# A streaming encoder on one core: own buffers for the `up` copies, constants loaded in the mixers, and corrected durations in the order planner

## The chip, the cores and the metric

The kernel runs on one core of one Trainium2 chip. The metric is the device time of one execution in microseconds, lower is better. Three runs of the kernel before gave 2532.02, 2538.91 and 2546.72 us; the median, 2538.91, is the time before.

## What is computed

A two-layer encoder works on 576 token columns at once (512 of a prompt, 64 of a sample), all in 32-bit floats. Each layer has a gated feed-forward network (FFN), a token mixer and a second FFN, each with a modulated norm ahead of it and a gated residual behind it. In short:

```
for l in range(2):
    mod = (silu(c) @ ada_w[l] + ada_b[l])      # shift, scale, gate for 3 sub-layers
    x = x + 0.5 * gate * swiglu(norm(x), ff_w_in[l, 0], ff_w_out[l, 0])
    x = x + gate * mixer(norm(x))              # l = 0: gated delta rule + short conv
                                               # l = 1: stick-breaking attention
    x = x + 0.5 * gate * swiglu(norm(x), ff_w_in[l, 1], ff_w_out[l, 1])
y = rmsnorm(x)
swiglu(h) = (silu(h @ w_gate) * (h @ w_up)) @ w_out     # width 2816
```

The states and caches of both groups are outputs too.

## The kernel before

**Layout.** Activations are transposed: 128 features on the partitions, 576 token columns, in two halves of 288. A 32-bit product is made of three matmuls on split operands: the high part `wh` and the low part `wl` of a weight block, the high part `XH` and the low part `XL` of the activations (`wh XH + wh XL + wl XH`). In the FFN's second product the activations are `HH` and `HL`. One matmul has 128 x 128 weights and 288 columns. Weights come as `stage` tiles over the sync queue; ScalarE copies the high part, VectorE, GpSimd or an accumulating DMA makes the low part.

**Stages.** FFN 0, mixer 0 (four pairs of delta-rule heads, a chain of small matmuls per pair), FFN 1, FFN 2, mixer 1 (eight pairs of attention heads, nine query blocks each), FFN 3. In each FFN the 22 input steps come in three chunks of 8, 8 and 6, and after each chunk 8 output products, with a residual addition (`x<-d,mod,x`) on VectorE.

**Two kinds of input step.** A *whole step* (`dense`) makes gate and up of 128 hidden features with 2 x 8 blocks x 2 halves x 3 = 96 matmuls. A *step of seven* (`dense7`) makes the same with a scheme of seven block products, 7 x 4 x 3 = 84 matmuls, in the order P1, P2, P6, P5, P7, P3, P4; it needs sums of weight blocks (`ss`, VectorE) and sums of activations (`TH`, `TL`, made once per FFN by `t_task`). P1, P6, P7 and P4 accumulate on one PSUM bank with copies (`sg`, `up`) taken in between; P5 and P3 accumulate on another, and the copy of P5 is taken between them. `PLAIN` says how many steps of each FFN, from the first on, are whole.

**The buffers around the change.** In a step of seven, `evac7` copies P5 into the first half of an `hm` tile and P7 into the only `up` tile; `hm` has one buffer, and holds the product of gate and up of the step before until `HH` (ScalarE) and `HL` (VectorE) are made from it, which `late` puts into the next step, behind P6 and P5.

**Modulation.** The 2 x 72 columns of `mod` are products of a broadcast vector `cb` with rows of `ada_w`, on VectorE: a tile (`ada_tile`) is one 512 KB load `aw` over the sync queue into one of two buffers and two products `jk<-aw,cb` of 128 x 1024, one per group. `ada_task` gives out a tile every so many planned ns (6200 in FFN 0, 9500 in FFN 1 and 2) and not before the planned VectorE is nearly through.

**What sets the order.** The program is written out in the order in which a planner meets it. `Model` keeps a planned clock for each engine; `Eng.cost` gives each instruction a duration from its size. `Sched` holds tasks (the chains of the mixers, the norms, `t_task`, `ada_task`); after every third dense matmul `tick` runs the tasks whose time the planned TensorE clock has reached. A task gives back the planned time at which its data is ready. So the durations in `Eng.cost` decide behind how many dense matmuls each small step of a chain is placed, and where the modulation tiles stand on VectorE; each engine then runs its list strictly in that order. `S.until` and `S.finish` move the planned clock forward where the dense work needs a task's result.

All instructions are issued by one helper, line 191 of the profile, so groups are told apart by the tile names: `d` and `a` are PSUM tiles, `cm` holds the identity and the masks, `raw`, `kq`, `nat`, `uu`, `ot` belong to the delta chain, `qbH`, `kH`, `sg`, `cp`, `wt`, `vtk` to attention.

## Time and profile before

| | |
|---|---|
| median of three runs | 2538.91 us |
| the profiled execution, by its own time | 2543.82 us |
| its span in the profile | 2542.1 us |
| TensorE busy | 2377.7 us (94%) |
| VectorE busy | 1789.1 us (70%) |
| ScalarE busy | 1092.6 us (43%) |
| GpSimd busy | 340.5 us (13%) |
| mean granted clock of TensorE | 0.959 |

The profiled execution ran 4.9 us longer than the median of the runs. A busy share is the time between start and end of an engine's instructions; matmuls overlap, so a dense matmul shows about 300 ns although the next one starts much sooner. A wait of one engine costs time only where that engine sets the end; TensorE, in a list of its own, does so nearly everywhere. The granted clock has two levels, 1.0 (2.4 GHz) and 0.5 (1.2 GHz); a value between is a mean over a stretch.

### The profile page before, as it was taken

How to read it: one execution, taken by the hardware profiler on the slowest of the kernel's cores; microseconds unless marked ns; L12 is line 12 of the kernel's file. 1: busy time of each engine (PE TensorE's matmuls, PEld its weight loads, DVE VectorE, ACT ScalarE, POOL GpSimd, SP SyncE). 2: the span in 40 equal slices, each digit the busy share in tenths (PEclk: the TensorE clock that was granted, in tenths of full speed). 3: DMA queues.
4: the chain of work that ended last, by engine and by line, in shares of the span. 5: the costliest groups of instructions: out<-in, count | busy, mean ns of one | idle time of the engine just before them, and what ended most of it. 6: DMA issues, size and time to landing. Idle time of an engine off the chain costs nothing. (4 is left out here: it accounts for less than half of the span.)

```text
span 2542.1 us, 45405 instructions
## 1 busy us (share of the span) xinstructions
PE 2377.7 (94%) x18352; PEld 2287.6 (90%) x18352; DVE 1789.1 (70%) x3463; ACT 1092.6 (43%) x1990; POOL 340.5 (13%) x468
## 2 busy tenths in 40 slices
PE   6989899999888999999999999999988889999998
PEld 5989899998788999999999999999977879999998
DVE  7688978587686578686867756565576777848474
ACT  4434525453222255362544445354554445425252
POOL 4100000342122230000021000013000004000001
PEclk8989999998788999999999999999999989999999
DMA  6656655232123165464636544343544314423222
GB/s 237 191 163 175 191 178 150 88 109 57 45 58 104 44 164 158 145 188 150 174 107 174 150 113 136 100 117 109 159 127 128 105 63 137 127 83 100 92 88 75
DMA packets 107350, 321.55 MB, mean 126 GB/s; under 512 B 26066, under 2 KB 28370, under 8 KB 106884
## 3 DMA queue, kind: packets, MB, share of 16 engines
q1 hardware_dynamic: 95044, 273.02, 32.4%
q0 software_dynamic: 12096, 45.62, 9.7%
q8 instruction: 145, 2.38, 0.4%
q14 instruction: 65, 0.53, 0.1%
HBM read 261.47 MB, written 11.51 MB: 107 GB/s over the span
## 5 line engine op out<-in xcount | busy, mean ns | idle before, releaser
L191 PE MATMUL d<-XH,wh 128*128 128x288 f32 x2280 | 707.8, 310 | 53.5 <-ACT hm L191 36.5
L191 PE MATMUL d<-XL,wh 128*128 128x288 f32 x2280 | 690.9, 303 | 14.5 <-POOL XL L191 11.1
L191 PE MATMUL d<-XH,wl 128*128 128x288 f32 x2280 | 689.3, 302 | 7.8 <-DMA wl<-stage 6.1
L191 PEld LDWEIGHTS d<-XH,wh 128*128 128x128 f32 x2280 | 442.2, 194 | 74.3 <-ACT hm L191 43.0
L191 PEld LDWEIGHTS d<-XL,wh 128*128 128x128 f32 x2280 | 443.0, 194 | 22.1 <-POOL XL L191 17.6
L191 PEld LDWEIGHTS d<-XH,wl 128*128 128x128 f32 x2280 | 442.8, 194 | 9.7 <-DMA wl<-stage 7.3
L191 PE MATMUL d<-HL,wh 128*128 128x288 f32 x1408 | 416.6, 296 | 2.1 <-DVE HL L191 1.9
L191 PE MATMUL d<-HH,wh 128*128 128x288 f32 x1408 | 416.5, 296 | 0.2 <-ACT HH L191 0.2
L191 ACT ACTIVATE wh<-stage 128x1024 fp32r<-128x1024 f32 (+3 forms) x345 | 319.6, 939 | 224.6 <-PE d L191 207.4
L191 PE MATMUL d<-HH,wl 128*128 128x288 f32 x1408 | 414.3, 294 | 0.0
L191 DVE TENSOR_TENSOR wl<-stage,wh 128x1024 fp32r<-128x1024 f32 (+3 forms) x258 | 267.6, 1042 | 133.0 <-ACT wh L191 130.7
L191 DVE SCALAR_TENSOR_TENSOR jk<-aw,cb 128x1024 fp8e4<-128x1024 f32 x256 | 315.5, 1232 | 42.2 <-DMA aw<-in_ada 37.8
L191 PE MATMUL d<-TH,wh 128*128 128x288 f32 x1072 | 318.8, 297 | 10.8 <-ACT sg L191 10.4
L191 PE MATMUL d<-TL,wh 128*128 128x288 f32 x1072 | 318.4, 297 | 0.0
L191 PE MATMUL d<-TH,wl 128*128 128x288 f32 x1072 | 318.2, 297 | 0.0
L191 DVE SCALAR_TENSOR_TENSOR x<-d,mod,x 128x64 f32<-128x64 f32 (+2 forms) x384 | 146.6, 413 | 220.3 <-PE d L191 219.5
L191 PEld LDWEIGHTS d<-HL,wh 128*128 128x128 f32 x1408 | 264.4, 188 | 4.4 <-DVE HL L191 4.4
L191 PEld LDWEIGHTS d<-HH,wh 128*128 128x128 f32 x1408 | 264.4, 188 | 0.4 <-ACT HH L191 0.4
L191 PEld LDWEIGHTS d<-HH,wl 128*128 128x128 f32 x1408 | 264.6, 188 | 0.0
L191 PEld LDWEIGHTS d<-TH,wh 128*128 128x128 f32 x1072 | 203.5, 190 | 14.0 <-ACT sg L191 13.8
L191 PEld LDWEIGHTS d<-TH,wl 128*128 128x128 f32 x1072 | 203.6, 190 | 0.1
L191 PEld LDWEIGHTS d<-TL,wh 128*128 128x128 f32 x1072 | 203.5, 190 | 0.0
(329 smaller groups left out, 3480.2 us busy)
## 6 DMA issues: line engine op xcount, KB each, us to landing
stage<-in_w SPq DMA_DIRECT2D x301, 512.0 KB, 3.6
aw<-in_ada SPq DMA_DIRECT2D x128, 512.0 KB, 4.4
wl<-stage POOLq DMA_DIRECT2D x60, 512.0 KB, 4.7
stage<-in_w SPq DMA_DIRECT2D x36, 384.0 KB, 2.9
TL<-XL POOLq DMA_DIRECT2D x8, 576.0 KB, 8.0
TL<-ss POOLq DMA_DIRECT2D x8, 576.0 KB, 5.8
TL<-in_ada SPq DMA_DIRECT2D x8, 512.0 KB, 10.0
stage<-in_w SPq DMA_DIRECT2D x8, 320.0 KB, 3.6
```

Of the source, the lines that this page charges most:

```text
L191: r = real(*args, **kw)
```

## The change

The P5 copy of a step of seven goes into a tile of `up`, which has two buffers now, and no longer into `hm`; the ring of `hf` in the norms has five tiles in place of four. The room comes from `cm`, which keeps only the identity; the four masks of the delta chain are loaded at the start of mixer 0 (`cmx`), and the visibility mask at the start of mixer 1 (`vis`), and what is made from them is made in their tasks. FFN 0 has seven whole steps in place of six. In `Eng.cost` a dense matmul of n columns takes 0.4576 n + 0.7 ns (132.5 for 288) in place of 0.417 n + 3 (123.1), with a floor of 110, and a modulation product of 1024 takes 1.04 n + 240 (1305) in place of 1.04 n + 65 (1130).

```
--- before.py
+++ after.py
@@ -44,7 +44,7 @@
 PK = ((1,5),(0,1))
 LOLAG = 0
 DSH = ((2, 4, 6), (1, 4, 6))
-PLAIN = (6, 5, 5, 5)
+PLAIN = (7, 5, 5, 5)
 EVEN_ODD = (0, 2, 4, 6, 1, 3, 5, 7)
 
 
@@ -208,14 +208,14 @@
                 return 107.0
             if ins[0].dtype == F32:
                 return max(27.0, n * 1.667)
-            return max(107.0, n * 0.417 + 3.0)
+            return max(110.0, n * 0.4576 + 0.7)
         if self.name == "ACT":
             return n * 0.833 + (51.0 if ps else 95.0)
         if self.name == "POOL":
             if op == "tensor_tensor" or op in ("tensor_mul", "tensor_add", "tensor_sub"):
                 return n * 2.1 + 90.0
             return n * 1.0 + 90.0
-        f = 130.0 if any(Model.size(x) == 1 for x in ins) and n > 1 else 65.0
+        f = 240.0 if op == "scalar_tensor_tensor" and n == D else 130.0 if any(Model.size(x) == 1 for x in ins) and n > 1 else 65.0
         if op == "tensor_reduce":
             n = Model.size(ins[0])
         if op == "reciprocal":
@@ -336,7 +336,7 @@
     NSM = a["small"].shape[1]
     x = base.tile([P, 8, NT], F32, name="x")
     small = base.tile([P, NSM], F32, name="small")
-    cm = base.tile([P, 6, P], F32, name="cm")
+    cm = base.tile([P, 1, P], F32, name="cm")
     XH = Quarters(base.tile([P, 2, 2, 4, 288], F32R, name="XH"))
     XL = Quarters(base.tile([P, 2, 2, 4, 288], F32R, name="XL"))
     cb = base.tile([P, 2, D], F32, name="cb")
@@ -345,7 +345,7 @@
     V.memset(ones, 1.0)
     dma(small, a["small"])
     dma(cm[:, 0], a["cm"][:, 0])
-    ident, Ule, Lgt, Ulb, Lgb, vis = (cm[:, i, :] for i in range(6))
+    ident = cm[:, 0]
     sm = {}
     c0 = 0
     for n, sh in SMALL:
@@ -726,7 +726,7 @@
     def modulated(pool, l, s, dsh=DSH):
         def out(kt, half, r):
             t0 = HALF[half][0]
-            u = pool.tile([P, 288], F32, name="hf", bufs=4)
+            u = pool.tile([P, 288], F32, name="hf", bufs=5)
             for c0, c1, g in GROUPS[half]:
                 V.scalar_tensor_tensor(u[:, c0 - t0:c1 - t0], x[:, kt, c0:c1], mod[:, l, s * 3 + 1, kt, g:g + 1],
                                        r[:, c0 - t0:c1 - t0], op0=OP.mult, op1=OP.mult)
@@ -877,11 +877,10 @@
                 if step == "P6":
                     g[1] = copy("sg", ps, 3)
                 if step == "P5":
-                    up[0] = pool.tile([P, NT], F32, name="hm")[:, :288]
-                    A.activation(up[0], ps, AF.Copy)
+                    up[0] = copy("up", ps, 2)
                     A.activation(g[0], g[0], AF.Silu)
                 if step == "P7":
-                    up[1] = copy("up", ps, 1)
+                    up[1] = copy("up", ps, 2)
                 if step == "P3":
                     V.tensor_sub(up[1], up[0], up[1])
                     V.tensor_sub(g[1], ps, g[1])
@@ -902,7 +901,7 @@
                         gate[half] = pool.tile([P, 288], F32, name="sg", bufs=3)
                         A.activation(gate[half], ps, AF.Silu)
                     else:
-                        h = pool.tile([P, 288], F32, name="up") if half else pool.tile([P, NT], F32, name="hm")[:, :288]
+                        h = pool.tile([P, 288], F32, name="up", bufs=2) if half else pool.tile([P, NT], F32, name="hm")[:, :288]
                         V.tensor_mul(h, gate[half], ps)
                         A.activation(HH[:, jj, t0:t1], h, AF.Copy)
                         V.tensor_sub(HL[:, jj, t0:t1], h, HH[:, jj, t0:t1].bitcast(F32))
@@ -936,8 +935,9 @@
         gl = pool.tile([P, 5, 8], F32R, name="gl")
         LgtR = pool.tile([P, P], F32R, name="LgtR")
         LgbR = pool.tile([P, P], F32R, name="LgbR")
-        A.activation(LgtR, Lgt, AF.Copy)
-        A.activation(LgbR, Lgb, AF.Copy)
+        cmx = pool.tile([P, 4, P], F32, name="cmx")
+        dma(cmx, a["cm"][:, 1:5])
+        Ule, Lgt, Ulb, Lgb = (cmx[:, i] for i in range(4))
         EG = pool.tile([P, 3, 5, 8], F32, name="EG")
         B9 = pool.tile([P, 3, 4, 9], F32, name="B9")
         gs = pool.tile([P, 2, 4], F32, name="gs")
@@ -948,6 +948,8 @@
 
         def ab_task(ab):
             yield M.ready(ab[:64, 0:NT])
+            A.activation(LgtR, Lgt, AF.Copy)
+            A.activation(LgbR, Lgb, AF.Copy)
             pt = psum.tile([P, 5, 64], F32, name="a")
             for u in range(5):
                 c = u * P
@@ -1511,8 +1513,8 @@
             for h in range(2):
                 r, c = slice(h * 64, h * 64 + 64), slice(64 - h * 64, 128 - h * 64)
                 V.tensor_copy(qb[r, :, c], zf[r, None, :].to_broadcast([64, 9, 64]))
-        visb = vis[:, 0:64]
-        V.tensor_scalar(hide, visb, 1e30, -1e30, op0=OP.mult, op1=OP.add)
+        visb = pool.tile([P, 64], F32, name="vis")
+        dma(visb, a["cm"][:, 5, 0:64])
         att_tasks = []
         qkv = {}
         hs = (slice(0, 64), slice(64, 128))
@@ -1521,6 +1523,8 @@
             while p and not att_tasks[p - 1][2]:
                 yield S.clock + 300.0
             yield M.ready(qf, kf, vf)
+            if p == 0:
+                V.tensor_scalar(hide, visb, 1e30, -1e30, op0=OP.mult, op1=OP.add)
             ck = pool.tile([P, NPR], F32, name="ck")
             dma(ck, a["ck"][p])
             vc = pool.tile([P, 4, P], F32, name="vc")
@@ -1783,7 +1787,6 @@
                 paused[0] = False
                 for _ in range(2):
                     w_dma()
-                dma(cm[:, 1:], a["cm"][:, 1:])
 
         feed.scales = scales, scales_out, scales_end
         task = feed
```

The new durations move instructions on all engines. Three places follow.

VectorE in FFN 0, where the whole steps end and the sums for the first step of seven begin (`jk` modulation tiles, `TL` activation sums, `ss` weight sums); before:

```order
L191 SCALAR_TENSOR_TENSOR jk,mod<-aw,cb 128x1024 x2
L191 TENSOR_TENSOR up<-sg,d 128x288
L191 TENSOR_TENSOR HL<-up,HH 128x288
L191 SCALAR_TENSOR_TENSOR jk,mod<-aw,cb 128x1024 x2
L191 TENSOR_TENSOR TL<-ss,TH 128x1152
L191 TENSOR_TENSOR TL<-TL,TH 128x1152
L191 SCALAR_TENSOR_TENSOR jk,mod<-aw,cb 128x1024 x2
L191 TENSOR_TENSOR TL<-TL,TH 128x1152
L191 TENSOR_TENSOR ss<-stage 128x512
L191 TENSOR_TENSOR ss<-ss,stage 128x512
L191 SCALAR_TENSOR_TENSOR jk,mod<-aw,cb 128x1024 x2
L191 TENSOR_TENSOR hm<-sg,d 128x288
```

and now:

```order
L191 SCALAR_TENSOR_TENSOR jk,mod<-aw,cb 128x1024 x2
L191 TENSOR_TENSOR up<-sg,d 128x288
L191 TENSOR_TENSOR HL<-up,HH 128x288
L191 TENSOR_TENSOR wl<-stage,wh 128x1024
L191 SCALAR_TENSOR_TENSOR jk,mod<-aw,cb 128x1024 x2
L191 TENSOR_TENSOR TL<-ss,TH 128x1152
L191 TENSOR_TENSOR TL<-TL,TH 128x1152
L191 TENSOR_TENSOR hm<-sg,d 128x288
L191 TENSOR_TENSOR HL<-hm,HH 128x288
L191 TENSOR_TENSOR wl<-stage,wh 128x1024
L191 SCALAR_TENSOR_TENSOR jk,mod<-aw,cb 128x1024 x2
L191 TENSOR_TENSOR TL<-TL,TH 128x1152
```

Three tiles and three `TL` parts stood between an `HL` and the next product `hm<-sg,d`; now one tile and at most two `TL` parts stand between two products, and a whole step more lies in between. In the second chunk of FFN 0 the eight steps of seven hold 15 tiles in place of 14.

TensorE in mixer 0, at the end of the first pair's delta chain: `uu` goes into the state and output products, `ot` is their result after VectorE's norm, and `cm,ot` are its transposes. Before:

```order
L191 MATMUL d<-XH,wh 128x288
L191 MATMUL d<-XL,wh 128x288
L191 MATMUL d<-XH,wl 128x288
L191 MATMUL a<-Sb,kq 128x128 x2
L191 MATMUL a<-xr,nat 128x64 x2
L191 MATMUL a<-uu,ktok 128x128
L191 MATMUL a<-uu,DM_5540 128x64
L191 MATMUL a<-uu,DM_5552 128x64
L191 MATMUL a<-iT,nat 32x16 x36
L191 MATMUL a<-cm,ot 128x128 x4
L191 MATMUL a<-cm,ot 64x64 x2
```

and now, the rows that end with the transposes:

```order
L191 MATMUL d<-XH,wh 128x288
L191 MATMUL d<-XL,wh 128x288
L191 MATMUL d<-XH,wl 128x288
L191 MATMUL a<-iT,nat 32x16 x36
L191 MATMUL d<-XH,wh 128x288
L191 MATMUL d<-XL,wh 128x288
L191 MATMUL d<-XH,wl 128x288
L191 MATMUL d<-XH,wh 128x288
L191 MATMUL d<-XL,wh 128x288
L191 MATMUL d<-XH,wl 128x288
L191 MATMUL a<-cm,ot 128x128 x4
L191 MATMUL a<-cm,ot 64x64 x2
```

Before, nothing dense stood between the last `uu` products and the transposes of `ot`; now 30 dense matmuls do. At the third pair's end there were none either, and there are 51 now.

TensorE in mixer 1, in the last attention pair (`kH,qbH` to `kH,qbL` are the scores of a block, `cm,sg` transposes of the weights). Before, two blocks of it:

```order
L191 MATMUL a<-kH,qbH 128x128
L191 MATMUL a<-hide,idR 128x64
L191 MATMUL a<-kL,qbH 128x128
L191 MATMUL a<-kH,qbL 128x128
L191 MATMUL a<-cm,sg 64x128
L191 MATMUL a<-kH,qbH 128x192
L191 MATMUL a<-hide,idR 128x64
L191 MATMUL a<-kL,qbH 128x192
L191 MATMUL a<-kH,qbL 128x192
```

and now, the same two blocks:

```order
L191 MATMUL a<-kH,qbH 128x128
L191 MATMUL a<-hide,idR 128x64
L191 MATMUL a<-kL,qbH 128x128
L191 MATMUL a<-kH,qbL 128x128
L191 MATMUL a<-cm,sg 64x128
L191 MATMUL d<-XH,wh 128x288
L191 MATMUL d<-XL,wh 128x288
L191 MATMUL d<-XH,wl 128x288
L191 MATMUL a<-kH,qbH 128x192
L191 MATMUL a<-hide,idR 128x64
L191 MATMUL a<-kL,qbH 128x192
L191 MATMUL a<-kH,qbL 128x192
```

Before, no dense matmul was left when the last pair began. Now the pair begins 72 dense matmuls earlier, and they stand between its steps.

## Rows read from the trace of the kernel before

**Rows 1.** The page: span, and busy us of each engine.

```profile
span 2542.1 us, 45405 instructions
...
PE 2377.7 (94%) x18352; PEld 2287.6 (90%) x18352; DVE 1789.1 (70%) x3463; ACT 1092.6 (43%) x1990; POOL 340.5 (13%) x468
```

**Rows 2.** PE's waits, whole span: who was waited for, us, times, longest us.

```profile
PE d L191 <- ACT hm L191: 36.5, 26, 4.3
...
PE a L191 <- DVE ot L191: 11.3, 2, 6.2
...
PE d L191 <- POOL XL L191: 11.1, 18, 1.3
```

**Rows 3.** ACT's groups: busy us, mean ns, idle before, releasers.

```profile
L191 ACT ACTIVATE hm<-d 128x288 f32<-128x288 f32 x67 | 27.6, 412 | 103.6 <-DVE HL L191 95.7 <-PE d L191 7.9
```

**Rows 4.** PE on hm: 150-219, 219-326, 326-450, 880-1100, 1100-1300, 1300-1720, 2100-2543 us.

```profile
PE d L191 <- ACT hm L191: 4.3, 1, 4.3
...
PE d L191 <- ACT hm L191: 9.0, 7, 1.7
...
PE d L191 <- ACT hm L191: 3.7, 3, 1.6
...
PE d L191 <- ACT hm L191: 4.0, 1, 4.0
...
PE d L191 <- ACT hm L191: 7.1, 6, 1.8
...
PE d L191 <- ACT hm L191: 4.8, 4, 1.3
...
PE d L191 <- ACT hm L191: 3.7, 4, 1.3
```

**Rows 5.** Timeline, 115 to 163 us: start, length, engine, instruction, idle before.

```profile
115.22 18.21 SPq L327 DMA_DIRECT2D aw<-in_ada  x5
...
129.57 0.61 PE L191 MATMUL d<-XH,wl 128*128 128x288 f32 x1 [4.06 <-DMA wl<-stage]
...
140.04 0.61 PE L191 MATMUL d<-TH,wh 128*128 128x288 f32 x1 [4.95 <-ACT sg L191]
...
162.83 0.61 PE L191 MATMUL d<-XH,wh 128*128 128x288 f32 x1 [4.32 <-ACT hm L191]
```

**Rows 6.** Stretches: us, busy and (count) of PE, PEld, DVE, ACT, POOL, clock, DMA.

```profile
130.00:135.00 5.00, 5.00 (x22) 4.86 (x21) 4.46 (x9) 1.52 (x3) 0.00 (x0) 0.52 0.31 104
...
140.00:145.00 5.00, 4.96 (x20) 4.96 (x21) 2.93 (x5) 3.77 (x5) 0.81 (x1) 0.50 0.58 206
...
160.00:170.00 10.00, 7.17 (x33) 7.17 (x34) 7.98 (x15) 2.68 (x6) 0.00 (x0) 0.66 0.74 262
```

**Rows 7.** The same view, a stretch of unbroken dense products.

```profile
1500.00:1600.00 100.00, 98.62 (x740) 97.90 (x739) 62.72 (x100) 52.14 (x84) 5.09 (x6) 1.00 0.49 132
```

**Rows 8.** DVE's modulation products, 224.06 to 312.92 us, and that stretch.

```profile
L191 DVE SCALAR_TENSOR_TENSOR jk<-aw,cb 128x1024 fp8e4<-128x1024 f32 x26 | 31.8, 1222 | 0.5
...
224.06:312.92 88.86, 80.80 (x591) 78.64 (x590) 86.07 (x147) 48.49 (x83) 6.07 (x7) 1.00 0.69 202
```

**Rows 9.** Timeline of PE, one wait, and the stretch 1000 to 1010.

```profile
1005.60 0.61 PE L191 MATMUL d<-XH,wh 128*128 128x288 f32 x1 [4.00 <-ACT hm L191]
...
1000.00:1010.00 10.00, 6.00 (x36) 5.76 (x35) 7.37 (x13) 2.83 (x6) 0.00 (x0) 0.83 0.57 165
```

**Rows 10.** Timeline of PE in mixer 0: the two long waits.

```profile
657.00 1.53 PE L191 MATMUL a<-cm,ot 128*128 128x128 f32 x8 [5.13 <-DVE ot L191]
...
820.10 1.52 PE L191 MATMUL a<-cm,ot 128*128 128x128 f32 x8 [6.15 <-DVE ot L191]
```

**Rows 11.** Timeline of PE, end of mixer 1, and a stretch of it.

```profile
2067.71 0.30 PE L191 MATMUL a<-kH,qbH 128*128 128x64 f32 x1 [1.48 <-ACT qbH L191]
...
2076.09 1.55 PE L191 MATMUL a<-wt,vtk 128*64 128x256 f32 x8 [0.80 <-ACT wt L191]
...
2070.00:2080.00 10.00, 8.27 (x36) 6.69 (x36) 4.72 (x16) 3.94 (x13) 0.00 (x0) 0.51 0.00 0
```

More of the change, by code (lines that the diff above doesn't have):

```diff
@@ L46 @@
 DSH = ((2, 4, 6), (1, 4, 6))
-PLAIN = (6, 5, 5, 5)
+PLAIN = (7, 5, 5, 5)
 EVEN_ODD = (0, 2, 4, 6, 1, 3, 5, 7)
@@ L210, in cost @@
                 return max(27.0, n * 1.667)
-            return max(107.0, n * 0.417 + 3.0)
+            return max(110.0, n * 0.4576 + 0.7)
         if self.name == "ACT":
@@ L217, in cost @@
             return n * 1.0 + 90.0
-        f = 130.0 if any(Model.size(x) == 1 for x in ins) and n > 1 else 65.0
+        f = 240.0 if op == "scalar_tensor_tensor" and n == D else 130.0 if any(Model.size(x) == 1 for x in ins) and n > 1 else 65.0
         if op == "tensor_reduce":
@@ L338, in encoder_step @@
     small = base.tile([P, NSM], F32, name="small")
-    cm = base.tile([P, 6, P], F32, name="cm")
+    cm = base.tile([P, 1, P], F32, name="cm")
     XH = Quarters(base.tile([P, 2, 2, 4, 288], F32R, name="XH"))
@@ L347, in encoder_step @@
     dma(cm[:, 0], a["cm"][:, 0])
-    ident, Ule, Lgt, Ulb, Lgb, vis = (cm[:, i, :] for i in range(6))
+    ident = cm[:, 0]
     sm = {}
@@ L728, in out @@
             t0 = HALF[half][0]
-            u = pool.tile([P, 288], F32, name="hf", bufs=4)
+            u = pool.tile([P, 288], F32, name="hf", bufs=5)
             for c0, c1, g in GROUPS[half]:
@@ L879, in evac @@
                 if step == "P5":
-                    up[0] = pool.tile([P, NT], F32, name="hm")[:, :288]
-                    A.activation(up[0], ps, AF.Copy)
+                    up[0] = copy("up", ps, 2)
                     A.activation(g[0], g[0], AF.Silu)
                 if step == "P7":
-                    up[1] = copy("up", ps, 1)
+                    up[1] = copy("up", ps, 2)
                 if step == "P3":
@@ L904, in evac @@
                     else:
-                        h = pool.tile([P, 288], F32, name="up") if half else pool.tile([P, NT], F32, name="hm")[:, :288]
+                        h = pool.tile([P, 288], F32, name="up", bufs=2) if half else pool.tile([P, NT], F32, name="hm")[:, :288]
                         V.tensor_mul(h, gate[half], ps)
@@ L938, in mixer0 @@
         LgbR = pool.tile([P, P], F32R, name="LgbR")
-        A.activation(LgtR, Lgt, AF.Copy)
-        A.activation(LgbR, Lgb, AF.Copy)
+        cmx = pool.tile([P, 4, P], F32, name="cmx")
+        dma(cmx, a["cm"][:, 1:5])
+        Ule, Lgt, Ulb, Lgb = (cmx[:, i] for i in range(4))
         EG = pool.tile([P, 3, 5, 8], F32, name="EG")
@@ L950, in ab_task @@
             yield M.ready(ab[:64, 0:NT])
+            A.activation(LgtR, Lgt, AF.Copy)
+            A.activation(LgbR, Lgb, AF.Copy)
             pt = psum.tile([P, 5, 64], F32, name="a")
@@ L1513, in mixer1 @@
                 V.tensor_copy(qb[r, :, c], zf[r, None, :].to_broadcast([64, 9, 64]))
-        visb = vis[:, 0:64]
-        V.tensor_scalar(hide, visb, 1e30, -1e30, op0=OP.mult, op1=OP.add)
+        visb = pool.tile([P, 64], F32, name="vis")
+        dma(visb, a["cm"][:, 5, 0:64])
         att_tasks = []
@@ L1523, in att_pair @@
             yield M.ready(qf, kf, vf)
+            if p == 0:
+                V.tensor_scalar(hide, visb, 1e30, -1e30, op0=OP.mult, op1=OP.add)
             ck = pool.tile([P, NPR], F32, name="ck")
@@ L1785, in feed @@
                     w_dma()
-                dma(cm[:, 1:], a["cm"][:, 1:])
         feed.scales = scales, scales_out, scales_end
```

## The prediction

> **What bounds the kernel now.** I read the page first. TensorE is busy 2377.7 of 2542.1 us, 94% [rows 1]; the other engines matter only where they make it wait or let its clock fall. So the time to be had is TensorE's idle time, 164 us, and the matmuls that ran at half clock. The profiled execution took 2543.8 us by the clock outside, 4.9 us above the median of the three runs, 2538.9; the sum is made against 2543.8 and its difference is carried over to the median. Half a percent, 12.7 us, is about what a measurement of this kernel can tell from no change.
>
> Second, who is waited for. The largest single entry is the copy of a product into `hm` by ScalarE: 36.5 us in 26 waits, the longest 4.3 [rows 2]. ScalarE itself is idle 103.6 us before that copy, 95.7 of it for VectorE's `HL` [rows 3]. This is one chain: in a step of seven products the copy of P5 goes into the only `hm` buffer, which the step before still needs until `HL` is made from it; P3 accumulates onto the bank that this copy has to empty, and P3 comes one product (12 matmuls) after P5. A late `HL` thus stops TensorE although nothing of the step needs `HL`. By stretch the waits are 4.3, 9.0, 3.7, 4.0, 7.1, 4.8 and 3.7 us [rows 4].
>
> Third, the time line where the first FFN passes from whole products to steps of seven. TensorE waits 4.06, 4.95 and 4.32 us there, for a low weight part, for an `sg` copy and for `hm` [rows 5], and after each the clock is granted at half, 1.2 in place of 2.4 GHz [rows 6]. All three have one origin: VectorE is behind, because the order gives it three modulation tiles and three `TL` parts between one `HL` and the next product (the order rows). The sync queue, too, stands 18.2 us at five `aw` loads whose buffers VectorE hasn't freed [rows 5], with the weights queued behind them.
>
> Fourth, what a dense matmul takes: 98.62 us busy for 740 of them in a full stretch, 133.3 ns from one to the next [rows 7]. The planner's table had 0.417 x 288 + 3 = 123.1 ns and gets 0.4576 x 288 + 0.7 = 132.5. A modulation product takes 1222 ns [rows 8]; the table had 1024 x 1.04 + 65 = 1130 and gets 1305.
>
> **The change part by part.** All gains are in us against 2543.8.
>
> *A, the entry into the first steps of seven.* Waits 4.06 + 4.95 + 4.32 = 13.3. Half clock: 5.00 - 22 x 0.1333 = 2.1, 4.96 - 20 x 0.1333 = 2.3 and 7.17 - 33 x 0.1333 = 2.8 [rows 6], together 7.1. So 20.4 at most. In the new order each product of a whole step stands between two modulation tiles, the `TL` parts are spread over one more step, and chunk 0 has one step of seven, which removes the third wait with its `hm`. The least it could give is the third wait and its clock, 4.3 + 2.8 = 7. I take 17, near the upper end, since two of the three causes are gone from the order and the third is thinner.
>
> *B, one whole step more* (PLAIN 6 to 7): 96 matmuls in place of 84, 12 x 0.1333 = 1.6 lost. Its two low weight parts replace four sums and the low parts of a step of seven on VectorE; that is counted in A.
>
> *C, own buffers for the two `up` copies.* The copy of P5 then waits for TensorE and for its place in ScalarE's queue alone. What is late next: `HL` and, right behind it on VectorE, the low part of the fourth weight combination, which P4 needs, one product after P3. So lateness of VectorE is forgiven for about one product more, 12 x 0.1333 = 1.6 us. The short waits are 1.3 to 1.8 each [rows 4], so most are covered: 3.7 + 4.0 + 7.1 + 4.8 + 3.7 = 23.3 in the stretches after 326 us. The 4.0 one is a modulation tile standing between the weight part and `HL`; the new order has that tile ahead of both. Bounds 6 and 23.3; I take 80%, 18.6, plus 6.00 - 36 x 0.1333 = 1.2 for the clock after the 4.0 [rows 9]: 19.8.
>
> The 9.0 of 219 to 326 us I leave out. There VectorE is busy 86.1 of 88.9 us [rows 8]: 26 modulation products in seven steps are more than it can do in 591 x 0.1333 = 78.8 us of matmuls, so a freed buffer only shifts the wait. The new order has one tile more in that chunk, 2 x 1.22 = 2.4 lost at worst; at best, 9.0 gained. I take 0.
>
> *D, mixer 0.* The two long waits, 5.13 and 6.15 [rows 10], stand where the old order puts the transposes of `ot` right behind the matmuls that `ot` is made from. The new one puts 30 and 51 dense matmuls between, 4.0 and 6.8 us. That removes 4.0 + 6.15 = 10.2; but elsewhere in the chain the new order has steps closer to each other, for which I take off 2: 8. Bounds 2 and 11.3.
>
> *E, the end of mixer 1.* The last attention pair runs alone in the old order, with five waits from 1.48 to 0.80, 4.2 together, in its first half and the clock at 0.51 [rows 11]. The new order has 72 dense matmuls, 9.6 us, between its steps. Bounds 0 and 4.2 + 0.49 x 8.27 = 8.3; I take 6.
>
> *F, what the corrected clock of the planner costs.* It now counts 7.6% more time for each dense matmul, so every small step of the mixers is set behind fewer of them, nearer to when its data is ready. Some will come a little too early. Bounds 0 and 12 (as much as the two long waits of D, which are such a step set too early); I take 6.
>
> *At nothing:* the constants. The upper five leave the start (no row there waits for them), four come at the start of mixer 0 into the place where the first FFN's `TH` lay, which the last 24 output steps of that FFN don't read; the last comes in mixer 1 likewise. The sync queue could stand at such a load, with weights behind it, only if TensorE were still in the steps of seven. The moved ScalarE copies of two 128 x 128 constants lie in a task that waits anyway. A fifth `hf` buffer could help only in the norms, where TensorE waits 11.1 us for `XL` [rows 2]; that wait is for GpSimd's subtractions, which stay as they are, so nothing.
>
> Sum: 17 - 1.6 + 19.8 + 0 + 8 + 6 - 6 = 43.2. That is 2500.6 for the profiled execution and 2495.7, say **2496**, for the median.
>
> A rule against the change: the Trainium skill ("TensorE: Matmul & The Clock Gate", section "Wait — 56ns, not 53.3ns?") gives N / 2.4 GHz + 2.5 ns from one warm matmul to the next, by which 288 columns would take an estimated 122.5 ns, the old entry would be right, and only A, B and C would stay: 2538.9 - 35.2 = 2504. The trace doesn't agree: 133.3 ns at a granted clock of 1.00 [rows 7].
>
> **The rivals.** *The wait changes its name* (0.20). VectorE's lateness lasts longer than one more product, and P4 waits for the low weight part where P3 waited for `hm`. For it: 9.0 us in a stretch that VectorE fills [rows 4, 8]. Against: after 326 us the waits are single and short. C falls to 6, and the time is 2496 + 14 = 2510.
>
> *VectorE binds at the entry too* (0.11). If the tiles, now also at a shorter true interval, keep it behind there, A gives 7, C 6, D and E 7 together, less 1.6 and 6: 12.4, and 2527, within half a percent.
>
> *The planner runs slow, the mixers wait* (0.07; slower). With 7.6% fewer dense matmuls per planned microsecond the steps of the attention pairs (8 pairs of 9 blocks, two dependent steps each, 144) and of the four delta pairs (some 30 each, 120) reach TensorE before VectorE and ScalarE are done. The waits at steps with nothing between are 0.80 and 1.48 [rows 11]. If each of the 264 waits 0.25 us more, 66 us are lost against the other 49 gained: 2539 + 17 = 2556. It turns slower than before from 0.19 a step. Against it: the dense matmuls do take 133.3 ns, so the new clock is the true one. The skill's rule above would make this rival the likely one, if it held here.
>
> **How the numbers follow.** Forecast 0.62, with 2480 to 2512 as its own range; the rivals 0.20, 0.11 and 0.07. All upper bounds together (20.4 + 24.5 + 9.0 + 11.3 + 8.3 - 1.6 = 71.9) give 2467, all lower ones about 2540. The range 2472 to 2530 leaves out the last rival, part of the second, and the sum of all best cases. Faster by over 0.5% (below 2526): forecast and first rival less a little, 0.80; within: 0.13; slower: 0.07.
>
> **What would show it.** In the changed profile TensorE's wait for `hm` is gone, and what waits for an `up` copy stays under 10 us; between 100 and 170 us no wait over 2 us and the clock at 1.00; 1100 to 1300 without hm-like waits; no wait for `ot` over 2 us; the end of mixer 1 shorter by some 6 us; a wait on `wl` or `HL` in the second chunk of the first FFN about as long as the 9.0 before. Wrong would be: waits on `wl` that add up to what `hm` had (first rival), or waits on `sg`, `wt`, `xr`, `uu` in the mixers that grow by tens of us (the last).

## The result, and the profile after

The changed kernel took 2475.63 us (2472.78 to 2480.11) where the kernel before took 2542.81 us (2532.02 to 2547.66) on the same chip: a ratio of 0.9743, interval 0.9705 to 0.9781, 67 us less. The profiled executions have spans of 2475.6 and 2542.1 us, a difference of 66.5 that the rest accounts for.

The page of the changed kernel, to be read against [rows 1]:

```profile
span 2475.6 us, 45399 instructions
...
PE 2358.8 (95%) x18364; PEld 2278.5 (92%) x18364; DVE 1784.2 (72%) x3456; ACT 1091.2 (44%) x1984; POOL 339.6 (14%) x467
```

TensorE has 12 matmuls more and is busy 18.9 us less, so it ran more of them at full clock (its mean granted clock is 0.969 in place of 0.959); its idle time fell from 164.4 to 116.8 us. The list of what TensorE waited for, whole span (us, times, longest), shows where; `hm`, first in [rows 2] with 36.5, is no longer in it:

```profile
PE d L191 <- ACT sg L191: 13.2, 15, 2.3
PE d L191 <- POOL XL L191: 8.0, 15, 0.7
PE a L191 <- DVE sg L191: 7.1, 11, 1.5
PE a L191 <- ACT raw L191: 6.7, 2, 4.0
...
PE a L191 <- DVE t2k L191: 5.5, 5, 2.2
PE a L191 <- DVE ot L191: 4.4, 3, 1.8
...
PE d L191 <- ACT wh L191: 3.9, 1, 3.9
...
PE d L191 <- DVE wl L191: 1.7, 4, 0.7
```

By stage. A stage is cut at the first matmul of the norm that leads into the next one, so the stretches are the first FFN (from 75 us on), mixer 0, FFN 1, FFN 2, mixer 1, FFN 3. Columns: stretch, its length, TensorE busy (matmuls), granted clock, DMA share, GB/s. Before:

```profile
75.00:479.78 404.78, 375.38 (x2731) 0.97 0.57 172
479.78:888.64 408.86, 380.86 (x3666) 0.89 0.23 70
888.64:1315.87 427.23, 408.51 (x3026) 0.99 0.54 158
1315.87:1728.54 412.67, 402.23 (x3002) 1.00 0.47 128
1728.54:2109.01 380.47, 342.18 (x2478) 0.93 0.38 116
2109.01:2523.22 414.21, 403.87 (x3003) 0.99 0.33 100
```

And after:

```profile
75.00:466.33 391.33, 374.20 (x2739) 0.98 0.58 176
466.33:873.50 407.17, 379.90 (x3667) 0.90 0.24 71
873.50:1286.76 413.26, 405.65 (x3026) 1.00 0.56 166
1286.76:1692.81 406.05, 402.21 (x3002) 0.99 0.47 127
1692.81:2048.48 355.67, 329.08 (x2478) 0.96 0.41 124
2048.48:2456.91 408.43, 401.08 (x3003) 1.00 0.33 101
```

The gains are 13.5, 1.7, 14.0, 6.6, 24.8 and 5.8 us, and 0.2 in the end. The largest is in mixer 1, where the prediction had 6; mixer 0, where it had 8, gave next to nothing.

### The profile page after: what moved, and what is told of

Same layout as the page of the kernel before. It is cut to its first block, busy times and chain, and to the rows that moved or that the text cites. A ratio compares the mean times of both kernels' runs of the same rounds, so it can differ in the third digit from the quotient of the medians.

```text
span 2475.6 us, 45399 instructions
## 1 busy us (share of the span) xinstructions
PE 2358.8 (95%) x18364; PEld 2278.5 (92%) x18364; DVE 1784.2 (72%) x3456; ACT 1091.2 (44%) x1984; POOL 339.6 (14%) x467
## 5 line engine op out<-in xcount | busy, mean ns | idle before, releaser
L191 PE MATMUL d<-XL,wh 128*128 128x288 f32 x2304 | 697.0, 303 | 11.3 <-POOL XL L191 8.0
L191 PEld LDWEIGHTS d<-XH,wh 128*128 128x128 f32 x2304 | 447.3, 194 | 27.4 <-ACT XH L191 11.3
L191 PE MATMUL d<-TH,wh 128*128 128x288 f32 x1056 | 312.1, 296 | 12.8 <-ACT sg L191 12.7
L191 PE MATMUL d<-TL,wh 128*128 128x288 f32 x1056 | 312.2, 296 | 0.0
L191 PE MATMUL d<-TH,wl 128*128 128x288 f32 x1056 | 311.9, 295 | 0.2
L191 PEld LDWEIGHTS d<-TL,wh 128*128 128x128 f32 x1056 | 198.3, 188 | 0.0
```

The source lines that it names most:

```text
L191: r = real(*args, **kw)
```

## The experiments

Twelve kernels. All stage lengths below are cut at the same matmuls as above (FFN 0 from 0 us). In the FFNs, where an edit leaves the order alone, they repeat within 3.5 us. In the mixers one order spreads more: the nine kernels with the changed kernel's order in mixer 0 (changed, e3, e5, e6, e9 to e13) lie between 401.2 and 412.9 there, and before and e1, with one order on TensorE in mixer 1, take 380.5 and 374.4 for it. These spreads are the resolution of the table. A stage length is that of one profiled execution, which isn't the median: e1's was the shortest of its four, 9.3 us under its median, and e4's the longest, 10.2 over.

| kernel | us (ratio to before, interval) | FFN 0 | mixer 0 | FFN 1 | FFN 2 | mixer 1 | FFN 3 |
|---|---|---|---|---|---|---|---|
| before | 2542.81 | 479.8 | 408.9 | 427.2 | 412.7 | 380.5 | 414.2 |
| changed | 2475.63 (0.9743, 0.9705 to 0.9781) | 466.3 | 407.2 | 413.3 | 406.0 | 355.7 | 408.4 |
| e1 | 2515.45 (0.9889, 0.9849 to 0.9929) | 473.6 | 404.5 | 416.0 | 407.0 | 374.4 | 409.8 |
| e2 | 2519.69 (0.9912, 0.9881 to 0.9942) | 484.6 | 409.6 | 425.8 | 410.8 | 353.5 | 413.5 |
| e3 | 2481.56 (0.9756, 0.9737 to 0.9776) | 475.7 | 402.0 | 412.9 | 406.1 | 352.2 | 410.3 |
| e4 | 2516.41 (0.9899, 0.9869 to 0.9928) | 467.6 | 404.6 | 421.9 | 406.8 | 391.5 | 413.7 |
| e5 | 2474.70 (0.9742, 0.9715 to 0.9769) | 464.4 | 406.5 | 412.2 | 408.6 | 355.5 | 408.6 |
| e6 | 2501.43 (0.9846, 0.9814 to 0.9878) | 463.9 | 408.2 | 413.1 | 407.3 | 384.5 | 409.0 |
| e7 | 2513.89 (0.9899, 0.9865 to 0.9934) | 468.8 | 425.2 | 421.2 | 406.7 | 359.3 | 408.3 |
| e9 | 2493.26 (0.9811, 0.9784 to 0.9838) | 464.7 | 403.5 | 412.8 | 406.0 | 379.3 | 408.5 |
| e10 | 2479.92 (0.9768, 0.9747 to 0.9789) | 462.8 | 412.9 | 413.9 | 405.0 | 357.3 | 409.4 |
| e11 | 2486.38 (0.9797, 0.9771 to 0.9824) | 465.6 | 401.2 | 412.6 | 406.1 | 368.9 | 409.0 |
| e12 | 2472.85 (0.9743, 0.9726 to 0.9759) | 464.4 | 408.0 | 412.8 | 406.0 | 351.8 | 408.7 |
| e13 | 2495.14 (0.9813, 0.9789 to 0.9837) | 467.4 | 407.1 | 425.9 | 410.1 | 352.8 | 412.7 |

### The four parts alone: e1 to e4

e1 is the changed kernel with all planner numbers of before, so only the buffers and the constants are new:

```diff
-PLAIN = (7, 5, 5, 5)
+PLAIN = (6, 5, 5, 5)
-            return max(110.0, n * 0.4576 + 0.7)
+            return max(107.0, n * 0.417 + 3.0)
-        f = 240.0 if op == "scalar_tensor_tensor" and n == D else 130.0 if any(...
+        f = 130.0 if any(...
```

> The own up buffers, the fifth hf and the constants in the mixers, with the old durations and six whole steps, so with the order of the kernel before. Theory 1 (the parts add up: the hm wait is a buffer's doing, mixer 1 is the planner's): TensorE's wait for hm is gone, the first FFNs gain, the mixers stay as they were (mixer 1 some 380 us): about 2515 us, 25 to 30 under the kernel before. Theory 2 (the waits came from the order, and a buffer only gives the wait another name): VectorE is as late as before, P4 or the next sg copy waits instead, and the time stays within 10 us of before, 2533 or more.

It came to 0.9889, and FFN 1 to 3 gained 11.2, 5.7 and 4.4 us. The wait for `hm` is gone, but over the whole span `wl` rises from 1.6 to 9.9 us and `sg` from 11.0 to 17.3, so with the old order part of the wait does change its name, 14.6 of the 36.5 us by these two rows. The opposite, e2, is the kernel before with the two corrected times alone:

```diff
-            return max(107.0, n * 0.417 + 3.0)
+            return max(110.0, n * 0.4576 + 0.7)
-        f = 130.0 if any(...
+        f = 240.0 if op == "scalar_tensor_tensor" and n == D else 130.0 if any(...
```

> The corrected durations alone: one hm and one up buffer, all constants at the start, six whole steps. Theory 1: mixer 1 takes about 356 us as in the changed kernel, the hm wait stays near 36 us: about 2517 us. Theory 2: hm waits fall below 12 us because VectorE's list is in the right order now, and the time is 2495 or less.

0.9912. The order alone doesn't touch the `hm` wait, which stays the longest row of its list (against 36.5 in [rows 2]):

```profile
PE d L191 <- ACT hm L191: 38.5, 25, 4.3
```

but it shortens mixer 1 by 27.0 us, all that the whole change does there. So the two parts act in different stages. In the profiled executions they add up: 37.6 us for e1 and 25.2 for e2, and 63.5 for e3 below, which has both. By the medians it is 27.9, 23.7 and 61.8, since e1's lies above its profiled execution. The theory that a buffer only renames the wait falls. In FFN 0 the table alone costs 4.8 us, a little more than the spread.

e3 is the changed kernel with `PLAIN` at 6:

> The changed kernel with six whole steps in the first FFN. VectorE's list then has three modulation tiles before the first step of seven again, as before. Theory 1 (the entry is cured by the whole step more): two waits of 4 to 5 us with a half clock behind each come back between 120 and 150 us, less 1.6 us for the matmuls saved: some 2488 us, 10 to 13 slower than the changed kernel. Rival (the right durations cure the entry, the step only costs 1.6 us): 2474, no slower than the changed kernel.

Between the two expectations: 0.9756 against 0.9743, intervals that overlap. By stage FFN 0 is 9.3 us longer, so the seventh whole step does clear the entry. Mixer 0 is 5.2 and mixer 1 3.5 shorter; TensorE has the same order in both, so this is spread.

e4 is the changed kernel with the old matmul time:

```diff
-            return max(110.0, n * 0.4576 + 0.7)
+            return max(107.0, n * 0.417 + 3.0)
```

> The changed kernel with the old duration of a dense product, 123.1 ns for 288 columns; the modulation product keeps 1305. The order puts the last attention pair behind all but none of the dense matmuls again, and nothing dense between uu and ot in mixer 0. Theory 1: mixer 1 goes back to about 380 us, mixer 0 stays within 5 us of 407: 2500 us, some 25 slower than the changed kernel. Rival (mixer 1 gained by something else, such as the mask loaded there or the buffers): mixer 1 stays near 356 and the time within 6 us of the changed kernel.

It lost more than expected: mixer 1 takes 391.5 us, 35.8 more, with FFN 1 and FFN 3 8.7 and 5.3 longer. The stage lengths are of its longest execution, and what lengthened these two FFNs wasn't followed up.

### The modulation time, and mixer 1 alone: e5 and e6

e5 puts only the modulation time back (`f = 130.0`, 1130 ns):

> The changed kernel with the planner's old time for a modulation product (1130 ns in place of 1305), all else as changed. Theory 'true pace' (each of the two corrected times repairs the stages in which that work is dense): the modulation tiles crowd the first FFN again, so its length goes from 391 us (75 us to its end) to about 400, with waits behind VectorE between 100 and 330 us, while the second mixer stays near its 356 us: 2486 in all. Rival 'one knob' (both corrections only slow the planned clock, the matmul's does nearly all): no stage changes by more than 3 us, 2476 to 2479.

No difference, 0.9742, and no stage moves by more than 2.5 us. This correction, by itself, is worth nothing.

e6 uses the old matmul time only while mixer 1 is laid out:

```diff
-            return max(110.0, n * 0.4576 + 0.7)
+            return max(107.0, n * 0.417 + 3.0) if self.m.old else max(110.0, n * 0.4576 + 0.7)
...
+        M.old = True
         task = mixer1(mp, task, npool, at)
+        M.old = False
```

> The changed kernel with the old time of a dense matmul (123.1 ns) used only while the second mixer is laid out, 132.5 ns everywhere else. Theory 'true pace': what the second mixer gained is a matter of its own plan, so it goes from 356 us back to 375 to 391 us (what it took with the old time everywhere) and every other stage stays within 3 us: 2495 to 2511. Rival 'what comes before it' (the mixer gained because the FFN ahead leaves its tiles and loads in a better place): the second mixer stays within 5 us of 356, 2474 to 2481.

Mixer 1 goes back to 384.5 us, every other stage stays within 2.5. So mixer 1's gain is made in its own plan and by the matmul time, not by where the FFN ahead left its tiles.

### What the matmul time does in mixer 1

Of its eight attention pairs, take the fifth. Its last two blocks before, from the time line of TensorE (start, length, instruction, what it waited for):

```profile
1965.01 0.63 PE L191 MATMUL a<-cm,sg 128*128 128x128 f32 x4 [0.53 <-DVE sg L191]
...
1969.37 1.09 PE L191 MATMUL a<-cm,sg 128*128 128x128 f32 x4 [2.66 <-DVE sg L191]
1971.14 3.25 PE L191 MATMUL a<-wt,vtk 128*64 128x256 f32 x16 [0.69 <-ACT wt L191]
```

and the same place after:

```profile
1918.65 0.63 PE L191 MATMUL a<-cm,sg 128*128 128x128 f32 x4
...
1921.84 0.63 PE L191 MATMUL a<-cm,sg 128*128 128x128 f32 x4 [0.22 <-ACT sn L191]
...
1923.16 1.74 PE L191 MATMUL a<-wt,vtk 128*64 128x256 f32 x16 [0.29 <-ACT wt L191]
```

Before, no dense matmul stands between these steps: TensorE waits 2.66 us for VectorE, and then the same 16 matmuls take 3.25 us in place of 1.74. After, between the rows shown, three dense ones stand ahead of the next scores, six ahead of the second transposes and three ahead of the value products. And the clock, columns as by stage, around these steps before and after:

```profile
1969.00:1975.00 6.00, 4.95 (x25) 0.53 0.17 68
```

```profile
1918.00:1927.00 9.00, 7.77 (x70) 1.00 0.25 91
```

Behind the bare waits it is granted at half, 1.2 in place of 2.4 GHz. Both pairs hold the same 120 dense matmuls: in every kernel without a ration (below) the second to fifth pair hold 168, 120, 168 and 120, the projections that the next pair waits for. The planner lays this supply out greedily, in each gap as many as fit, by its table, into the time that it thinks the data takes. The fourth pair shows it, counted from the time lines. Dense matmuls ahead of each group; S scores, T transposes, P value products, waits over 0.3 us in brackets. The rows show 165 of the 168; three more follow the last step:

```
before  69S 18S 0T 3S 3T 3S 3T 3S 15T 6P 0S 0T 3S 39T 0S 0T 0S 0T(1.5) 0P(0.7) 0T 0P(0.5) 0P(2.5)
changed 63S 15S 0T 3S 21T 3S 0T 3S 6T 6P 0S 0T 3S 33T 3S 0T 3S 3T(0.9) 0P(0.7) 0T 0P(0.6)
e6      69S 48S 0T 3S 3T 3S 3T 3S 3T 6P 0S 0T 3S 21T 0S 0T(0.8) 0S 0T(0.8) 0P(0.7) 0T 0P(0.6) 0P(0.8)
e10     69S 15S 15T 3S 0T 3S 6T(0.4) 3S 0T 9P 0S 0T 3S 9T 3S 15T(0.6) 3S 6T 3P 0T 0P(0.6)
```

With a time that is too short, all of these go ahead of the sixth block's transposes (39T, 21T), and the last blocks, whose scans on VectorE are the longest, have none; the changed kernel keeps 9 for them and e10 30. Mixer 1 cut at the second and the sixth pair's start, so the four middle pairs and, for the first two kernels, the rest (columns as by stage). Before:

```profile
1819.44:1977.15 157.71, 139.52 (x1030) 0.94 0.43 130
1977.15:2109.01 131.86, 117.43 (x833) 0.90 0.27 89
```

The changed kernel:

```profile
1784.77:1927.55 142.78, 133.11 (x1029) 0.98 0.47 143
1927.55:2048.48 120.93, 110.64 (x830) 0.94 0.30 97
```

e6:

```profile
1781.14:1947.75 166.61, 146.44 (x1031) 0.89 0.42 126
```

and e10, which comes below:

```profile
1781.35:1929.85 148.50, 133.31 (x1030) 0.99 0.45 134
```

From before to the changed kernel the four middle pairs gave 14.9 us and the last three with what follows 10.9. The matmuls are the same to a few records, yet busy time fell by 6.4 and 6.8, with the mean clock up by 0.04 in each: about half of the gain is the clock.

There is a rival that no run was made for: a modulation tile that stands on VectorE ahead of an awaited scan, or waits there for its own `aw` load, holds TensorE too, and its place moves with every plan. Counted from the time lines of both engines, TensorE's waits in mixer 1 that have such a tile in VectorE's work just ahead make 5.7 us before, 6.8 in e6 and 3.7 in the changed kernel. The difference is about a tenth of the gain, so this isn't what was gained here; in some kernels below it matters.

### True time, or a supply that lasts? e7, e9 to e12

e7 makes the matmul time 8% too long:

```diff
-            return max(110.0, n * 0.4576 + 0.7)
+            return max(118.0, n * 0.4942 + 0.7)
```

> The changed kernel with the planner's time of a dense matmul 8% too long (143.0 ns for 288 columns, measured 133.3). Theory 'true pace': small steps now stand behind fewer dense matmuls than their data needs, so the two mixers gain waits of 0.2 to 1 us each and lengthen by 5 to 15 us each: 2485 to 2500. Rival 'slower is better' (a slower planned clock keeps dense matmuls for the last pairs, whatever the true duration): the mixers stay or shorten further, 2465 to 2476.

2513.89: slower, as 'true pace' said, but not in the stage it said. Mixer 1 lost 3.6 us only; mixer 0 lost 18.0, more than its spread, and FFN 1 8.0. Of the 18.0 only 4.7 are idle time of TensorE; 13.3 are busy time, at a granted clock of 0.86 in place of 0.90. A longer time isn't better by itself.

e9 corrects one more time of the table, that of the scan:

```diff
+        if op == "tensor_tensor_scan":
+            return n * 2.08 + 150.0
```

> The changed kernel with one more planner time corrected: the scan on VectorE in the attention pairs, 2.08 n + 150 ns in place of 1.04 n + 65 (for 576 elements 1348 in place of 664; the trace of the changed kernel has 1344 for 576 and 689 for 256). The planner then lets more dense matmuls pass between a block's scores and its transposes. Theory 'true pace': TensorE's waits for sg in the second mixer fall from 7.1 us to under 3 and the clock there rises, so the mixer goes from 356 to 346 to 352 us: 2466 to 2472. Rival 'the reserve' (there are only so many dense matmuls; more of them early leaves the last pair bare): the sg waits move to the last pair, the mixer takes 356 to 370 us: 2476 to 2490.

'True pace' falls here: with a truer table the kernel is 0.7% slower, and mixer 1 takes 379.3 us. The longer planned scans draw more of the supply into the early gaps, and the second and the fourth pair end bare, the last has no dense matmul at all in its blocks, and the first row of waits is for the scan, which has no row in the changed kernel:

```profile
PE a L191 <- DVE cp L191: 12.3, 6, 4.4
```

Two of the six waits, 4.4 and 3.9 us, are more than a bare end: there VectorE has a modulation tile ahead of the scan, and waits 4.6 and 4.0 us for the tile's load.

So the spending was rationed directly. Wherever a block's scores have been issued, the planner waits for the sigmoid for 1.5 us at most:

```diff
-            yield M.ready(sgs[0])
+            yield min(M.ready(sgs[0]), S.clock + 1500.0)
...
-                    yield M.ready(sgs[i])
+                    yield min(M.ready(sgs[i]), S.clock + 1500.0)
```

e10 is e6, with its wrong time, and the ration:

> The kernel of e6 (old matmul time while the second mixer is laid out), with a ration: behind the scores of a block the planner waits at most 1.5 us (12 dense matmuls by its clock) for their sigmoid before it goes on to the next step. A pair of heads has a fixed supply of dense matmuls (168 or 120, the projections of the next pair); in e6 48 of them pass behind the first scores, and the last three blocks of five of the eight pairs stand bare. Theory 'supply spent early': with the ration one whole pair and the ends of two stay bare, so the second mixer falls from 384.5 to 355 to 367 us although its times are wrong, and the whole to 2472 to 2484. Rival 'true pace' (each step needs as many dense matmuls as its data takes, and the wrong time spoils that step by step): the ration sets steps too early as well, the waits grow, the mixer stays at 378 to 392, 2495 to 2510.

Mixer 1 takes 357.3 us: 27.2 of the 28.8 lost in e6 are back, with the matmul time still wrong (by the medians of the whole, 21.5 of 25.8). That decides between the two theories for this change: what the corrected time did in mixer 1 is to keep dense matmuls for the last blocks, and another way of keeping them does nearly as much.

e11 is the changed kernel with the ration:

> The changed kernel with the same ration of 1.5 us (11 dense matmuls by its clock) in the second mixer. 'Supply spent early': one pair (the fifth) still runs bare from its sixth block on, the last pair no longer does; the second mixer goes from 356 to 345 to 353 us, 2465 to 2473. Rival 'true pace': steps now come before their data, waits for sg and wt grow by 5 to 15 us, 2480 to 2490.

A miss: 2486.38, mixer 1 368.9, inside the range of 'true pace', and the waits for VectorE grew as that theory said. The fifth pair ran bare from its sixth block on, as expected; but it took 45.7 us in place of 31.7, with 24 more dense matmuls (3.2 us). The fourth pair lost 8.1 with 24 more, at waits of 5.6 us in place of 2.2. Three waits, in the second, fourth and fifth pair, of 3.4, 5.0 and 5.0 us, come to 13.4 together, and the stage lost 13.2. At each, VectorE has a modulation tile ahead of the awaited scan and waits for the tile's load itself. The one in the fourth pair, VectorE's row and then TensorE's:

```profile
1870.15 1.23 DVE L191 SCALAR_TENSOR_TENSOR jk<-aw,cb 128x1024 fp8e4<-128x1024 f32 x1 [5.91 <-DMA aw<-in_ada]
```

```profile
1874.07 0.87 PE L191 MATMUL a<-cm,sg 128*128 128x128 f32 x3 [5.04 <-DVE sg L191]
```

A ration of 1.5 us leaves no room for a tile, whose two products alone take 2.5. So the fifth pair doesn't show what a bare end costs; nearer to that is the fifth pair of e10, bare from about the same block on, with 120 dense matmuls: 39.0 us, 7.3 over the changed kernel's.

e12 is e9 with the ration:

> The kernel of e9 (the true time of the scan in the planner's table), which was slower by 18 us, with the same ration of 1.5 us. By the order no pair has a bare end left: between any two steps of the last blocks stand 3 to 12 dense matmuls. 'Supply spent early': what made e9 slow is gone, the second mixer takes 336 to 347 us, 2456 to 2467. Rival 'true pace': the ration undoes the truth that e9 brought, waits for sg return, and the mixer stays above 365 us, over 2484.

Mixer 1 falls from 379.3 to 351.8 us, so the bare ends, with the tiles in them, were what made e9 slow; but it misses the 336 to 347. No pair ends bare, and instead some steps right behind the ration come too early. The five longest, 1.9 to 4.0 us and 12.6 together, all have a modulation tile on VectorE just ahead; no step behind the ration without one waits over 0.7. Its first row of waits in mixer 1:

```profile
PE a L191 <- DVE sg L191: 13.0, 7, 4.0
```

The whole, 2472.85 us at 0.9743, is level with the changed kernel. No version here beats it by more than the measurement can tell.

### The buffers alone: e13

e13 is the changed kernel with both `up` copies back in the single buffers; on TensorE and VectorE the order is row for row the same:

```diff
-                    up[0] = copy("up", ps, 2)
+                    up[0] = pool.tile([P, NT], F32, name="hm")[:, :288]
+                    A.activation(up[0], ps, AF.Copy)
...
-                    up[1] = copy("up", ps, 2)
+                    up[1] = copy("up", ps, 1)
...
```

> The changed kernel with the copies of P5 and P7 put back into the single hm and the single up buffer, and nothing else: the order on TensorE and on VectorE is row for row that of the changed kernel, so whatever is lost is the wait on the buffers alone. Theory 'a buffer's wait' (the prediction's term C): TensorE waits for the copy into hm again, 25 to 40 us in all, the three later FFNs lengthen by 18 to 24 us together and the first by 3 to 8; the mixers stay within 3 us: 2496 to 2507. Rival 'the order had removed it' (with the corrected times VectorE is no longer late where hm was awaited): the hm waits stay under 10 us, 2476 to 2485.

2495.14, just under the first theory's range and far outside the rival's. The wait is back under its old name, with the order of the changed kernel; FFN 1, with 10.3 us of it, has the same busy time as the kernel before within 0.2 us, and 9.7 us more idle time than the changed kernel:

```profile
PE d L191 <- ACT hm L191: 28.3, 26, 2.1
...
874.41:1300.33 425.92, 408.64 (x3026) 0.99 0.54 161
```

FFN 1, 2 and 3 lost 12.7, 4.0 and 4.2 us, together 20.9; FFN 0 lost 1.0. By stage the wait is 9.7 us in FFN 0 and 10.3, 4.6 and 3.6 in FFN 1 to 3.

## Why the prediction was right, and where it was not

2496 was forecast, 2475.63 measured: right in sign, inside the range of 2472 to 2530, and the gain too small by 20 us. Most of that is one term, mixer 1, which a smaller miss in mixer 0 hides in part.

**C, the buffers: right in mechanism and size.** Forecast 19.8, and 20.9 in FFN 1 to 3 by e13. The wait was a buffer's, since the order without the buffer leaves it (e2, e13). In FFN 1 to 3 no other wait took the place of the 18.5 us that e13 has there, and `wl` is at 1.7 in all, so the first rival falls; with the old order it came true in part (`wl` 9.9 in e1). In FFN 0 the wait did change its name, to one that the rival hadn't named: 9.7 us for `hm` and 2.5 for `sg` in e13, 9.7 for `sg` in the changed kernel. About the 9.0 us between 219 and 326 us the prediction had said that VectorE binds there and that a freed buffer would only shift them. The waits of that stretch after:

```profile
PE d L191 <- ACT sg L191: 6.6, 8, 1.6
PE d L191 <- ACT HH L191: 1.7, 1, 1.7
PE d L191 <- DVE HL L191: 0.4, 1, 0.4
```

8.7 us where [rows 4] had 9.0, under the names of `sg` and `HH` in place of `wl` or `HL`; and e13 lost only 1.0 in all of FFN 0.

**A and B, the entry: the size nearly right, the cause half wrong.** 17 less 1.6 was forecast; FFN 0 gained 13.5, 12.5 of it not by the buffers. Two of the three waits of [rows 5] are gone, and about where the first stood there is one of the same length, for `wh`. VectorE's row, TensorE's, and the stretch around them:

```profile
124.58 1.23 DVE L191 SCALAR_TENSOR_TENSOR jk<-aw,cb 128x1024 fp8e4<-128x1024 f32 x1 [3.10 <-DMA aw<-in_ada]
```

```profile
131.47 0.61 PE L191 MATMUL d<-XH,wh 128*128 128x288 f32 x1 [3.92 <-ACT wh L191]
...
130.00:140.00 10.00, 8.12 (x39) 0.66 0.43 158
```

The prediction had said no wait over 2 us there and a clock of 1.00. The order would have allowed it: VectorE stands 3.10 us for the tile's load, and ScalarE's copy of the weights comes behind work that waits for VectorE. e6, e10 and e12 have the same order there and no wait for that load, and their longest wait between 100 and 170 us is 1.7; e9, e11 and e13 have both waits again. What lets the load come late in some executions isn't known. The prediction had put the waits before down to three modulation tiles in a row, which the corrected modulation time would spread. e5 has the old time and no wait over 2.0 us there, with FFN 0 at 464.4 us; e3 has the corrected one without the seventh whole step, two waits of 5.5 and 4.9 us, and 475.7. So the step did it, and the tile's time wasn't needed; VectorE's list in e3 has three tiles again where the changed kernel has one, which fits that the step makes room for the sums.

**D, mixer 0: the two waits fell, others took their place.** `ot` went from 11.3 us in two waits to 4.4, the longest 1.8, as said. It is the matmul time that did it: 10.8 in e1 and 10.7 in e4, both with the old time, 4.6 in e2, e3 and e5. But `t2k` rose from 1.7 to 5.5 us and `raw` from 4.8 to 6.7, and `x` with 3.3 is new. This last one stops the very transposes of `ot`, half way, so they still wait 7.7 us:

```profile
692.66 0.33 PE L191 MATMUL a<-cm,ot 64*64 64x64 f32 x4 [3.26 <-DVE x L191]
```

TensorE's idle time in the stage is 28.0 us before and 27.3 after. "For which I take off 2" was the step that was too small: mixer 0 gained 1.7, and over the nine kernels with this order its mean is 406.3 us, against 408.9 before and 404.5 in e1, which has the old order. That is nothing, within this stage's spread.

**E and F, mixer 1: the failed step.** The prediction saw only the last pair running alone and gave 6, with 8.3 as the bound; and it took 6 off both mixers together, since fewer dense matmuls behind each small step would set some too early. Measured, 24.8. The last three pairs with what follows gave 10.9, above the bound, and four pairs in the middle gave 14.9, to which no term pointed. The sign of F was wrong there: fewer dense matmuls in the early gaps aren't lost, they stand in the late ones. These pairs have 168 or 120 to spend, and e10 shows that how they are spread is what counts. The prediction counted them at the places where the diff of the orders was plain, and not along a whole pair.

**Not in the sum.** FFN 1 to 3 gained 26.4, 5.5 beyond the buffers. `XL` fell from 11.1 to 8.0 us, which the prediction had set at nothing. A full stretch runs at the same pace as before, the same window in the kernel before and then in the changed one:

```profile
1450.00:1550.00 100.00, 99.98 (x754) 1.00 0.46 117
```

```profile
1450.00:1550.00 100.00, 99.79 (x753) 1.00 0.52 137
```

100 us / 753 is 132.8 ns from one dense matmul to the next, 100 / 754 is 132.6; the 133.3 of [rows 7] came from a stretch with small gaps. The new table has 132.5.

**The rivals.** 'VectorE binds at the entry too' gave 2527: one wait stands there in some executions, no more. 'The planner runs slow, the mixers wait' (2556) fell for this change; e7, whose table really is too long, loses 18 us in mixer 0, but waits are only 4.7 of them and the clock makes the rest, which that rival hadn't counted. That rival was tied to the Trainium skill ("TensorE: Matmul & The Clock Gate", section "Wait — 56ns, not 53.3ns?"): by its N / 2.4 GHz + 2.5 ns, an estimated 122.5 ns for 288 columns, the old entry was the right one. The trace doesn't agree, with 132.8 ns at a granted clock of 1.00 over 753 matmuls. e4, with the old entry of 123.1 ns, was some 40 us slower; how much of that is the truth of the number and how much the way it spreads the supply is kept apart by e10 for mixer 1 alone: there it is the spread.

**Open.** Why the old matmul time lengthens FFN 1 by 8.7 us in e4 and by 2.7 in e1, which has it too: the one profile is of the longest execution and the other of the shortest, so the difference may be no more than that. And how much more mixer 1 holds, since the ration was tried at one length only and no run kept the modulation tiles away from it.

## What to carry to other kernels

Where independent matmuls are a fixed supply that fills the gaps of a chain, count them along the whole chain, gap by gap, to its last step: what a planner's table changes shows first in which gaps run dry, and a bare end costs its waits and about as much again in clock. A corrected duration helps if it makes the supply last and hurts if it draws on it sooner, true or not, so the spending is the thing to watch. One fixed ration isn't the cure either (e11): a step needs more where the engine that it waits for has something long, or something that itself waits for a load, ahead in its list. And a wait on a buffer stays through any change of order that doesn't free the buffer sooner: put the buffer back with the order held to price it.

## What the runs showed that was not expected

The scan on VectorE takes about twice as long per element as a product of the same size. VectorE's groups in mixer 1 of the changed kernel (busy us, mean ns):

```profile
L191 DVE TENSOR_TENSOR_SCAN cp<-sn,ones 128x576 f32<-128x576 f32 x8 | 10.8, 1344 | 0.0
...
L191 DVE TENSOR_TENSOR sg<-sg,cp 128x576 f32<-128x576 f32 x8 | 6.1, 758 | 0.3
...
L191 DVE TENSOR_TENSOR_SCAN cp<-sn,ones 128x256 f32<-128x256 f32 x8 | 5.5, 689 | 3.1 <-ACT sn L191 3.1
...
L191 DVE TENSOR_TENSOR sg<-sg,cp 128x256 f32<-128x256 f32 x8 | 3.4, 425 | 0.8
```

(1344 - 689) / 320 is 2.05 ns per element, (758 - 425) / 320 is 1.04. And what a late step costs is more than its wait: in the middle pairs of e6 the 1031 matmuls were busy 146.4 us, in the changed kernel 1029 were busy 133.1, so 13.3 of the 23.8 us between them are matmuls at the lower clock.

And a stage with one order and the same waits can still differ. Mixer 0 in e10 and in e11, whose edits lie in mixer 1 alone, has the same leading rows of waits (`t2k` 6.9, `raw` 6.7, `ot` 4.6 and 4.4), and these stretches:

```profile
462.79:875.67 412.88, 382.49 (x3666) 0.89 0.23 70
```

```profile
465.59:866.78 401.19, 372.65 (x3667) 0.91 0.24 72
```

9.8 of the 11.7 us lie in busy time, at a granted clock of 0.89 against 0.91. What decides between the two isn't known from these runs; it means that in mixer 0, with its many short gaps, a change of less than 12 us can't be told from one execution.
